# A two-block transformer forward on one core: scaling the pool weights and reordering the pool stage by hand, and two stacked norms from one power

## The chip, the cores and the metric

The kernel runs on one core of one Trainium2 chip. The metric is the device time of one execution in microseconds (us), the median over the runs shown. TensorE (PE) multiplies; VectorE (DVE), ScalarE (ACT) and GpSimd (POOL) work on tiles of 128 partitions; loads and stores are issued on the queue of SyncE (SP), a few on GpSimd's. The engines run at the same time and wait for each other by semaphores; each works through its own instructions in a fixed order, so an instruction that waits holds what stands behind it on the same engine.

## What is computed

256 tokens of 1024 numbers pass through two blocks. The first has a pooling layer and an attention layer, each followed by a gated feed-forward, and ends in an RMS norm. The second begins with a norm of its own, so two norms meet there.

```python
def rmsnorm(x, g):
    xf = x.astype(jnp.float32)
    y = xf * lax.rsqrt(jnp.mean(xf * xf, axis=-1, keepdims=True) + EPS)
    return (y * g.astype(jnp.float32)).astype(x.dtype)

def pool_mixer(h, w, scale):
    ...
    for g, win in enumerate(POOL_WINDOWS):          # (2, 4, 8, 16)
        ...
        outs.append(window_sum / cnt[None, :, None] - hf[:, :, sl])
    d = jnp.stack(outs, axis=2).astype(h.dtype)
    y = jnp.einsum('btgc,gce->btge', d, w).reshape(B, T, D)
    return y * scale

def first_block(x, norm_mixer, norm_ffn, pool_w, pool_scale, kv_norm, w_kv, w_q, w_o, rel_bias,
                w_gate_up, w_down, final_norm):
    ...
    for layer in range(DEPTH):                      # 2
        if layer < N_A_LAYERS:                      # 1
            x = x + pool_mixer(rmsnorm(x, norm_mixer[layer]), pool_w[layer], pool_scale[layer])
        else:
            ...
            x = x + o @ w_o[j]                      # attention
        x = x + swiglu(rmsnorm(x, norm_ffn[layer]), w_gate_up[layer], w_down[layer])
    return rmsnorm(x, final_norm)

def hybrid_layer(x, c, ...):                        # the second block
    ...
    h = rms_norm(x, norm1_g) * (1 + sc1) + sh1
    z = h @ w_in
    ...
```

The rest of the second block (sparse attention, a recurrent branch, a mixture of experts with 64 experts, a last norm) is not touched.

## The kernel before, in words

Tokens lie in two halves `t` of 128 partitions, `x_sb[:, t, :]`, and each half in two column halves `h` of 512. Large products are made in three parts: a weight is split into a high part `wH` (ScalarE copy, line 190 or 201) and a low part `wL` (a subtraction, line 191 on DVE, or line 202 on the engine that is handed in), the operand likewise (`hH`, `hL`), and `mm3` multiplies high by high, high by low, low by high (lines 206 to 208). Weights come into a ring of 1 MB buffers, `raw`, and a buffer can be loaded again once both parts of both column halves are split off.

The **pool stage** (lines 561 to 624) is the first stage. It loads `x`, the pooling matrix `am`, `vec` (gains and other columns), the pool weights `pw`, `k_base` (the identity for transposes), the first gate and up weights (`ffn0.load(0)`) and the scale row `psrow`, copied to all partitions, in this order on SP's queue. Then: the norm of each half (squares on ScalarE, two small DVE steps, a power to -0.5 on GpSimd that gives `rstd`, a scaling on DVE that gives `xn`); the pooling matmuls `pd`; their copies `dT` by ScalarE; the pool matmuls into `acc` (`pool_mm`); the update of `x_sb` (`pool_add`: multiply by `psrow`, add); the feed-forward's norm; transposes of `xn`; and the gain and split into `hH` (ScalarE) and `hL` (DVE) in `gain_split`. Here the order of ScalarE and DVE is as written (`manual_schedule`); that of TensorE, GpSimd and the queues is a planner's, which goes by its own estimates of time. `ffn0.prep(u, rest)` makes the high parts of unit `u` of the feed-forward (gate and up) and puts the low parts off into the list `rest`: entries 0 and 1 are unit 0, entries 2 and 3 unit 1. Before the change entries 0 and 1 run on DVE, 2 and 3 on GpSimd. `next(ada)` twice brings two of the matmuls of the second block's modulation between the transposes of the two halves.

The **feed-forward** (`Ffn.run`) goes through 22 units of 128 hidden columns: gate, up, the activation, and one unit later the product with `w_down` into four accumulators. Gate and up weights are loaded for two units at a time. `to_next` ends a stage: it adds the accumulators to `x_sb` (`upd`), takes the norm of each half, runs `mid` and transposes and spreads each half.

At the end of the **second feed-forward** (lines 739 to 804) both norms are made (`norm2`): sums of squares of `x`, the product `y` with the row `fr`, sums of squares of `y`, then two powers one after the other. Behind it stand the last modulation matmuls, `gains`, and a round trip of `gcol` and `bcol` through DRAM on GpSimd's queue (lines 801 to 804). GpSimd's next work there is loads and memsets for the second block, among them `ikz` (line 837), which the `pix` matmuls of line 899 need. `omu` (line 825) is a small DVE step on `vec` that the planner is free to place.

## Time and profile before

| | us |
|---|---|
| median of 3 runs | 1396.15 (1391.35 to 1396.72) |
| the profiled execution | 1396.91 |
| its span in the trace | 1394.8 |
| PE busy | 1338.2 (96%) |
| DVE busy | 743.8 (53%) |
| ACT busy | 548.3 (39%) |
| POOL busy | 118.8 (9%) |

An engine's busy time is a sum over the whole span, and PE matmuls overlap, so a PE at 96% is not a PE at its peak. A stage is read from the timeline of each engine over that stage: each row is a start, a duration, the instruction with what it writes and reads, and in brackets how long the engine was idle before it and what released it. The chain that ended last is the profile's own way back from the last instruction through what each step waited for.

### The profile page before, as it was taken

How to read it: one execution, taken by the hardware profiler on the slowest of the kernel's cores; microseconds unless marked ns; L12 is line 12 of the kernel's file. 1: busy time of each engine (PE TensorE's matmuls, PEld its weight loads, DVE VectorE, ACT ScalarE, POOL GpSimd, SP SyncE). 2: the span in 40 equal slices, each digit the busy share in tenths (PEclk: the TensorE clock that was granted, in tenths of full speed). 3: DMA queues.
4: the chain of work that ended last, by engine and by line, in shares of the span. 5: the costliest groups of instructions: out<-in, count | busy, mean ns of one | idle time of the engine just before them, and what ended most of it. 6: DMA issues, size and time to landing. Idle time of an engine off the chain costs nothing.

```text
span 1394.8 us, 22867 instructions
## 1 busy us (share of the span) xinstructions
PE 1338.2 (96%) x9151; PEld 1003.3 (72%) x9151; DVE 743.8 (53%) x1420; ACT 548.3 (39%) x1087; POOL 118.8 (9%) x158
## 2 busy tenths in 40 slices
PE   5999999999999998899999998899999999999996
PEld 4899997998799997789989888644545445445443
DVE  4656657565765555468777676533333343343333
ACT  4444445655544445365664543211221222222212
POOL 3010001000100002203342100300000000000000
PEclk9999999999999999899999998999999999999998
DMA  7887766652866646944411159499999999999993
GB/s 253 294 247 250 250 225 213 210 192 92 290 234 225 212 157 207 182 131 147 154 62 63 63 219 361 134 335 380 405 408 409 408 409 409 408 409 409 368 403 138
DMA packets 157312, 361.38 MB, mean 259 GB/s; under 512 B 9865, under 2 KB 92101, under 8 KB 153874
## 3 DMA queue, kind: packets, MB, share of 16 engines
q1 hardware_dynamic: 154674, 353.36, 70.0%
q0 software_dynamic: 2528, 6.51, 1.8%
q8 instruction: 75, 1.23, 0.4%
q14 instruction: 35, 0.29, 0.1%
HBM read 357.46 MB, written 2.37 MB: 258 GB/s over the span
## 4 chain that ended last, share of the span: by engine, by line
PE 79%; DMA 7%; issue 5%; DVE 5%; ACT 2%; POOL 1%; SPq 0%; POOLq 0%; ACTq 0%; DVEq 0%
PE pgu L1557 15%; PE pdn L1581 7%; PE pgu L206 5%; PE pgu L207 5%; PE pgu L208 5%; PE pxg L1524 4%; PE pz L206 4%; PE acc L1597 4%; PE pz L207 4%; PE pz L208 4%; PE acc L208 3%; PE acc L206 3%; PE acc L207 3%; DMA ew<-in_exp_up 3%; DMA raw<-in_w_gate_up 2%
## 5 line engine op out<-in xcount | busy, mean ns | idle before, releaser
L191 DVE TENSOR_TENSOR wL<-raw,wH 128x1024 fp32r<-128x1024 f32 (+1 forms) x229 | 270.7, 1186 | 200.2 <-ACT wH L190 199.4
L190 ACT ACTIVATE wH<-raw 128x1024 fp32r<-128x1024 f32 (+1 forms) x231 | 235.7, 1026 | 254.2 <-PE pgu L207 106.7
L207 PE MATMUL pgu<-hL,wH 128*128 128x256 f32 x704 | 198.1, 281 | 1.3 <-DVE hL L267 1.3
L206 PE MATMUL pgu<-hH,wH 128*128 128x256 f32 x704 | 198.0, 282 | 0.0
L208 PE MATMUL pgu<-hH,wL 128*128 128x256 f32 x704 | 198.0, 281 | 0.0
L207 PEld LDWEIGHTS pgu<-hL,wH 128*128 128x128 f32 x704 | 133.0, 189 | 3.5 <-DVE hL L267 1.7
L206 PEld LDWEIGHTS pgu<-hH,wH 128*128 128x128 f32 x704 | 132.7, 189 | 2.9 <-issue 0.6
L208 PEld LDWEIGHTS pgu<-hH,wL 128*128 128x128 f32 x704 | 133.0, 189 | 0.0
L206 PE MATMUL pz<-hH,wH 128*128 128x256 f32 x400 | 119.5, 299 | 3.3 <-ACT hH L190 2.6
L1557 PE MATMUL pgu<-ew,xx 128*64 128x512 f32 x512 | 117.8, 596 | 1.6 <-DMA ew<-in_exp_up 1.5
L1557 PE MATMUL pgu<-ew,xg 128*64 128x512 f32 x512 | 117.0, 596 | 0.4 <-DMA ew<-in_exp_up 0.4
L1581 PE MATMUL pdn<-ew,aT 128*64 128x512 f32 (+1 forms) x528 | 115.6, 580 | 0.0
L207 PE MATMUL pz<-hL,wH 128*128 128x256 f32 x400 | 114.3, 286 | 1.2 <-DVE hL L191 1.2
L208 PE MATMUL pz<-hH,wL 128*128 128x256 f32 x400 | 113.4, 284 | 0.0
L1581 PEld LDWEIGHTS pdn<-ew,aT 128*64 128x64 f32 x528 | 37.8, 137 | 72.1 <-issue 71.1
L1557 PEld LDWEIGHTS pgu<-ew,xx 128*64 128x64 f32 x512 | 36.2, 137 | 69.4 <-issue 66.1
L1557 PEld LDWEIGHTS pgu<-ew,xg 128*64 128x64 f32 x512 | 35.6, 137 | 67.4 <-issue 66.2
L1584 ACT ACTIVATE yH<-pdn 128x512 fp32r<-128x512 f32 (+1 forms) x66 | 38.5, 584 | 112.6 <-DVE pdn L1583 112.6
L206 PEld LDWEIGHTS pz<-hH,wH 128*128 128x128 f32 x400 | 76.6, 192 | 7.5 <-ACT hH L190 2.9
L207 PEld LDWEIGHTS pz<-hL,wH 128*128 128x128 f32 x400 | 76.7, 192 | 2.6 <-DVE hL L191 1.4
L208 PEld LDWEIGHTS pz<-hH,wL 128*128 128x128 f32 x400 | 76.6, 191 | 0.4 <-issue 0.3
L236 POOL TENSOR_TENSOR rstd<-ssv,mhalf 128x1 f32<-128x1 f32 x16 | 9.8, 614 | 768.0 <-DVE ssv L234 767.9
(408 smaller groups left out, 2528.1 us busy)
## 6 DMA issues: line engine op xcount, KB each, us to landing
ew<-in_exp_gate SPq DMA_DIRECT2D x128, 512.0 KB, 12.7
ew<-in_exp_up SPq DMA_DIRECT2D x128, 512.0 KB, 12.8
ew<-in_exp_down SPq DMA_DIRECT2D x64, 1024.0 KB, 12.1
raw<-in_w_gate_up SPq DMA_DIRECT2D x44, 1024.0 KB, 5.5
raw<-in_ada_w SPq DMA_DIRECT2D x24, 1024.0 KB, 5.0
raw<-in_w_in SPq DMA_DIRECT2D x23, 1024.0 KB, 5.3
raw<-in_w_down SPq DMA_DIRECT2D x22, 1024.0 KB, 5.3
raw<-in_w_kv SPq DMA_DIRECT2D x8, 1024.0 KB, 5.5
```

Source lines behind the costliest of these rows:

```text
L190: S.activation(dstH, src, AF.Copy)
L191: second.tensor_tensor(dstL, src, dstH.bitcast(F32), op=OP.subtract)
L206: PE.matmul(out_, lH, rH, start=first, stop=False)
L207: PE.matmul(out_, lH, rL, start=False, stop=False)
L208: PE.matmul(out_, lL, rH, start=False, stop=last)
L236: G.tensor_tensor(r, v, mhalf[:, 0:1], op=OP.pow)
L1524: PE.matmul(p[:, kk * w:kk * w + w], x[:, t, (kb + kk) * 128:(kb + kk) * 128 + 128], r, start=t == 0 and i == 0, stop=t == 1 and i == 1, s ...
L1557: PE.matmul(self.pg[64 * e:64 * e + 64, :].rearrange("p (i c) -> p i c", i=2), self.xg[:, k, 64 * e:64 * e + 64], self.W[e][k // 4][:, :, ...
L1581: PE.matmul(p[64 * e:64 * e + 64], self.aT[:, j, 64 * e:64 * e + 64], self.D[e][:, j, c:c + w], start=j == 0, stop=j == 1, skip_group_chec ...
L1584: S.activation(yH[:, sl], p, AF.Copy)
L1597: PE.matmul(self.ac[t][h][:, sl], l, self.y[h][i][:, sl], start=False, stop=i == 1 and self.last, skip_group_check=True)
```

## The change

Pool stage. The load of `psrow` moves from behind the gate/up loads to right behind `pw`. `pw` is multiplied by `psrow` in place, in two DVE instructions behind the second `xn`, so the accumulators hold the scaled result and the update of `x_sb` is one addition. ScalarE takes the squares of each half column by column behind its addition. The order is written out: both additions of half 0, the high parts of unit 0, its norm, then half 1's additions around the scaling of half 0, one low part, half 1's norm, both transposes; the high parts of unit 1 and the other three low parts follow behind these, all on DVE. `omu` is held behind the last low step of the last `gain_split`.

Second block. The update and the squares of `x` and `y` go by column halves as the accumulators come. Both norms come from one power over two columns: with v the mean square of `x` plus EPS, the second argument is the mean square of `y` over v, plus EPS.

```diff
-                    V.scalar_tensor_tensor(L[:, k, ts_], p[:, c], g(k), H[:, k, ts_].bitcast(F32), op0=OP.mult, op1=OP.subtract)
+                    last["gainL"] = V.scalar_tensor_tensor(L[:, k, ts_], p[:, c], g(k), H[:, k, ts_].bitcast(F32), op0=OP.mult, op1=OP.subtract).ins
...
         pw = wload(A["pool_w"].rearrange("o g (k p) e -> p (o g k) e", p=128), 8, 256)
+        psrow = wk.tile([128, D], F32, name="psrow")
+        DMA.dma_start(psrow, bcast(A["pool_scale"], D))
         K = consts(cp, "base")
         ident = K("ident")
         ffn0.load(0)
-        psrow = wk.tile([128, D], F32, name="psrow")
-        DMA.dma_start(psrow, bcast(A["pool_scale"], D))
...
+        pw = pw.rearrange("p (g k) e -> p g k e", k=2)
+        for k in range(2):
+            V.tensor_tensor(pw[:, :, k, :], pw[:, :, k, :], psrow.rearrange("p (g e) -> p g e", g=4), op=OP.mult)
...
-        def pool_add(t, h):
-            sl = x_sb[:, t, h * 512:(h + 1) * 512]
-            tmp = wk.tile([128, 512], F32, name="ptmp", bufs=2)
-            V.tensor_tensor(tmp, accs[t][h], psrow[:, h * 512:(h + 1) * 512], op=OP.mult)
-            V.tensor_tensor(sl, tmp, sl, op=OP.add)
-        rest = []
...
-        for t in range(2):
-            ffn0.prep(t, rest)
-            for h in range(2):
-                pool_add(t, h)
-                if t and not h:
-                    V.tensor_scalar(xn[:, 0, :], x_sb[:, 0, :], r0, None, op0=OP.mult)
-            sums = sumsq(x_sb[:, t, :], xn[:, t, :], "f0")
-            if t:
-                rest[1](V)
-                normed_t(1, xn, sums)
-                for f in rest[2:]:
-                    f(G)
-            else:
-                rest[0](V)
-                r0 = rsq(sums, "n")
-        for t in range(2):
-            if t:
-                with tc.issue_after(last["first"]):
-                    next(ada)
-                    next(ada)
-            transposed(xn, t, gain_split([(hH, hL, lambda k: vcol("nf0", k))], t))
+        rest, sums = [], [sm.tile([128, 2], F32, name="ss") for _ in range(2)]
+
+        def pool_add(t, h):
+            sl = slice(h * 512, (h + 1) * 512)
+            V.tensor_tensor(x_sb[:, t, sl], accs[t][h], x_sb[:, t, sl], op=OP.add)
+            S.activation(xn[:, t, sl], x_sb[:, t, sl], AF.Square, accum_out=sums[t][:, h:h + 1])
+
+        def scaled(t, r):
+            V.tensor_scalar(xn[:, t, :], x_sb[:, t, :], r, None, op0=OP.mult)
+        pool_add(0, 0)
+        pool_add(0, 1)
+        ffn0.prep(0, rest)
+        r0 = rsq(sums[0], "n")
+        pool_add(1, 0)
+        scaled(0, r0)
+        pool_add(1, 1)
+        rest[0](V)
+        r1 = rsq(sums[1], "n")
+        scaled(1, r1)
+        transposed(xn, 0, gain_split([(hH, hL, lambda k: vcol("nf0", k))], 0))
+        with tc.issue_after(last["first"]):
+            next(ada)
+            next(ada)
+        transposed(xn, 1, gain_split([(hH, hL, lambda k: vcol("nf0", k))], 1))
+        ffn0.prep(1, rest)
+        for f in rest[1:]:
+            f(V)
...
+        def upd2(t, h):
+
+            if not h:
+                ys.append(wk.tile([128, D], F32, name="y", bufs=2))
+                sums2.append([sm.tile([128, 2], F32, name="ss") for _ in range(2)])
+            sl = slice(h * 512, (h + 1) * 512)
+            add_acc(accs, t, h)
+            V.tensor_tensor(ys[t][:, sl], x_sb[:, t, sl], fr[:, sl], op=OP.mult)
+            for ss, src in zip(sums2[t], (x_sb[:, t, sl], ys[t][:, sl])):
+                S.activation(xn[:, t, sl], src, AF.Square, accum_out=ss[:, h:h + 1])
+
         def norm2(t):
 
-            y = wk.tile([128, D], F32, name="y", bufs=2)
-            s1 = sumsq(x_sb[:, t, :], xn[:, t, :], "fin")
-            V.tensor_tensor(y, x_sb[:, t, :], fr, op=OP.mult)
-            s2 = sumsq(y, xn[:, t, :], "w")
-            r1 = rsq(s1, "fin")
-            rr = sm.tile([128, 1], F32, name="rr")
-            V.tensor_tensor(rr, r1, r1, op=OP.mult)
-            V.tensor_scalar(s2, s2, rr, None, op0=OP.mult)
-            r2 = rsq(s2, "w")
-            V.tensor_scalar(xn[:, t, :], y, r1, r2, op0=OP.mult, op1=OP.mult)
-            S.activation(x_sb[:, t, :], y, AF.Copy, scale=r1)
+            y, vs = ys[t], wk.tile([128, 3], F32, name="vs2", bufs=2)
+            for i, ss in enumerate(sums2[t]):
+                V.tensor_scalar(vs[:, i:i + 1], ss[:, 0:1], ss[:, 1:2], 1.0 / D, op0=OP.add, op1=OP.mult)
+                if i:
+                    V.tensor_scalar(vs[:, 1:2], vs[:, 1:2], vs[:, 2:3], EPS, op0=OP.mult, op1=OP.add)
+                else:
+                    V.tensor_scalar(vs[:, 0:1], vs[:, 0:1], EPS, None, op0=OP.add)
+                    V.reciprocal(vs[:, 2:3], vs[:, 0:1])
+            rr = wk.tile([128, 2], F32, name="rr2", bufs=2)
+            G.tensor_tensor(rr, vs[:, 0:2], mhalf[:, 0:2], op=OP.pow)
+            V.tensor_scalar(xn[:, t, :], y, rr[:, 0:1], rr[:, 1:2], op0=OP.mult, op1=OP.mult)
+            S.activation(x_sb[:, t, :], y, AF.Copy, scale=rr[:, 0:1])
...
-            V.tensor_scalar(omu, vcol("mu"), -1.0, 1.0, op0=OP.mult, op1=OP.add)
+            with tc.issue_after(last["gainL"]):
+                V.tensor_scalar(omu, vcol("mu"), -1.0, 1.0, op0=OP.mult, op1=OP.add)
```

## Rows read from the trace of the kernel before

**Rows 1.** The page, part 4: the chain that ended last, shares by engine.

```profile
PE 79%; DMA 7%; issue 5%; DVE 5%; ACT 2%; POOL 1%; SPq 0%; POOLq 0%; ACTq 0%; DVEq 0%
```

**Rows 2.** Timeline of PE, 0 to 75 us: start, duration, instruction [idle before <-releaser].

```profile
14.44 0.66 PE L592 MATMUL acc<-raw,dT 128*128 128x256 f32 x2
...
18.93 4.05 PE L592 MATMUL acc<-raw,dT 128*128 128x256 f32 x18
29.79 1.94 PE L249 MATMUL pt<-k_base,xn 128*128 128x128 f32 x8 [6.81 <-DVE xn L609]
31.66 3.58 PE L513 MATMUL pada<-raw,silc 128*32 128x512 f32 x16
...
37.65 0.39 PE L207 MATMUL pgu<-hL,wH 128*128 128x256 f32 x1 [0.65 <-DVE hL L267]
...
52.56 0.28 PE L206 MATMUL pgu<-hH,wH 128*128 128x256 f32 x1
```

**Rows 3.** Waits of PE, 36 to 540 us: total, times, longest.

```profile
PE pt L249 <- DVE xn L241: 1.6, 2, 1.1
```

**Rows 4.** Timeline of DVE, 0 to 75 us.

```profile
7.98 0.17 DVE L825 TENSOR_SCALAR omu<-vec 128x14 f32<-128x14 f32 x1 [1.87 <-DMA vec<-in_vecs]
...
9.81 0.75 DVE L241 TENSOR_SCALAR xn<-x_sb,rstd 128x1024 f32<-128x1024 f32 x1 [0.67 <-POOL rstd L236]
18.92 0.69 DVE L598 TENSOR_TENSOR ptmp<-acc,psrow 128x512 f32<-128x512 f32 x1 [8.36 <-DMA psrow<-in_pool_scale]
19.64 0.69 DVE L599 TENSOR_TENSOR x_sb<-ptmp,x_sb 128x512 f32<-128x512 f32 x1
20.43 0.69 DVE L598 TENSOR_TENSOR ptmp<-acc,psrow 128x512 f32<-128x512 f32 x1
...
23.93 2.86 DVE L599 TENSOR_TENSOR x_sb<-ptmp,x_sb 128x512 f32<-128x512 f32 x1
...
32.97 2.30 DVE L241 TENSOR_SCALAR xn<-x_sb,rstd 128x1024 f32<-128x1024 f32 x1 [0.66 <-POOL rstd L236]
35.19 4.22 DVE L267 SCALAR_TENSOR_TENSOR hL<-pt,vec,hH 128x128 fp32r<-128x128 f32 x16
```

**Rows 5.** Timeline of POOL, 0 to 75 us.

```profile
6.19 0.56 POOL L236 TENSOR_TENSOR rstd<-ssv,mhalf 128x1 f32<-128x1 f32 x1 [2.67 <-DVE ssv L234]
...
23.89 5.09 POOL L202 TENSOR_TENSOR wL<-raw,wH 128x1024 fp32r<-128x1024 f32 x2
...
32.88 1.84 POOL L695 MEMSET qz<- 128x1024 f32 x2
```

**Rows 6.** The chain that ended last, 530 to 620 us: start, duration, what.

```profile
552.04 16.41 DMA gain_scr<-bcol
...
569.33 11.62 DMA gain_scr<-gcol
...
586.58 1.22 PE pix L899 x2
```

**Rows 7.** Waits of PE, 540 to 1395 us.

```profile
PE pix L899 <- ACT ikz L852: 4.1, 1, 4.1
```

**Rows 8.** The load of `pw`: SP's timeline, the issues (to landing), the stretch 10 to 12.

```profile
2.62 0.63 SPq L186 DMA_DIRECT2D raw<-in_pool_w  x1
...
raw<-in_pool_w SPq DMA_DIRECT2D x1, 1024.0 KB, 8.3
...
10.00:12.00 2.00, 1.51 (x7) 1.33 (x6) 0.56 (x1) 0.47 (x1) 0.00 (x0) 1.00 1.08 357
```

**Rows 9.** The page, part 5: low and high parts, busy us and mean ns.

```profile
L191 DVE TENSOR_TENSOR wL<-raw,wH 128x1024 fp32r<-128x1024 f32 (+1 forms) x229 | 270.7, 1186 | 200.2 <-ACT wH L190 199.4
L190 ACT ACTIVATE wH<-raw 128x1024 fp32r<-128x1024 f32 (+1 forms) x231 | 235.7, 1026 | 254.2 <-PE pgu L207 106.7
```

**Rows 10.** Windows: length, busy of PE, PEld, DVE, ACT, POOL, then PEclk, DMA, GB/s.

```profile
29.00:35.00 6.00, 5.21 (x24) 2.16 (x24) 5.27 (x7) 2.78 (x10) 2.33 (x3) 0.50 0.12 18
```

**Rows 11.** The page, part 6: gate/up loads, KB each, us to landing.

```profile
raw<-in_w_gate_up SPq DMA_DIRECT2D x44, 1024.0 KB, 5.5
```

More of the change, by code (lines that the diff above doesn't have):

```diff
@@ L592, in pool_mm @@
                     PE.matmul(accs[t][h][:, (g % 2) * 256:(g % 2) * 256 + 256], dT[:, 2 * g + kk, t * 128:(t + 1) * 128],
-                              pw[:, 2 * g + kk, :], start=kk == 0, stop=kk == 1)
-        def pool_add(t, h):
-            sl = x_sb[:, t, h * 512:(h + 1) * 512]
-            tmp = wk.tile([128, 512], F32, name="ptmp", bufs=2)
-            V.tensor_tensor(tmp, accs[t][h], psrow[:, h * 512:(h + 1) * 512], op=OP.mult)
-            V.tensor_tensor(sl, tmp, sl, op=OP.add)
-        rest = []
+                              pw[:, g, kk, :], start=kk == 0, stop=kk == 1)
         for t in range(2):
@@ L760, in build @@
         xn = xnorm(es)
-        def norm2(t):
-            y = wk.tile([128, D], F32, name="y", bufs=2)
-            s1 = sumsq(x_sb[:, t, :], xn[:, t, :], "fin")
-            V.tensor_tensor(y, x_sb[:, t, :], fr, op=OP.mult)
-            s2 = sumsq(y, xn[:, t, :], "w")
-            r1 = rsq(s1, "fin")
-            rr = sm.tile([128, 1], F32, name="rr")
-            V.tensor_tensor(rr, r1, r1, op=OP.mult)
-            V.tensor_scalar(s2, s2, rr, None, op0=OP.mult)
-            r2 = rsq(s2, "w")
-            V.tensor_scalar(xn[:, t, :], y, r1, r2, op0=OP.mult, op1=OP.mult)
-            S.activation(x_sb[:, t, :], y, AF.Copy, scale=r1)
+        ys, sums2 = [], []
+        def upd2(t, h):
[7 more added lines that the diff above has]
+                S.activation(xn[:, t, sl], src, AF.Square, accum_out=ss[:, h:h + 1])
+        def norm2(t):
+            y, vs = ys[t], wk.tile([128, 3], F32, name="vs2", bufs=2)
[10 more added lines that the diff above has]
+            S.activation(x_sb[:, t, :], y, AF.Copy, scale=rr[:, 0:1])
         def spread2(t):
@@ L793, in mid @@
             pa2.close()
-        to_next(tail, lambda t, h: add_acc(accs, t, h), norm2, spread2, ada, mid=mid)
+        to_next(tail, upd2, norm2, spread2, ada, mid=mid)
     for _ in ada:
```

## The prediction, made before the result was known

> **What bounds the kernel now.** I read the chain that ended last first: TensorE holds 79% of it, DVE 5%, DMA 7% [rows 1]. So an edit to DVE or GpSimd work pays only where TensorE waits for it, and the next view is TensorE's own waits. Up to 36 us TensorE has two holes [rows 2]: nothing before the first `xn` (8.8 us), and 6.81 us idle behind the last pool matmul until the normalised tile `xn` of line 609 comes. The first feed-forward matmul that runs without a break is the one at 37.65. From there to 540 us its listed waits are all short, 1.6 us at the most [rows 3]. Hence the time of that matmul sets the rest of the first block: what the pool stage gives up there arrives later one for one, since the loads behind it start when earlier buffers come free and move along.
>
> In the second hole DVE is the long engine. It waits 8.36 us for `psrow`, starts at 18.92 and then has no gap until 32 [rows 4]. Steps there are far longer than their own kind: the add at 23.93 takes 2.86 us where the one at 19.64 takes 0.69, the scaling at 32.97 takes 2.30 where the one at 9.81 takes 0.75. GpSimd runs at exactly these times: two low parts for 5.09 us, then two memsets of `qz` for 1.84 us [rows 5]. A DVE step that meets a long GpSimd step ends about when that ends.
>
> The second place of the change is the end of the second feed-forward, 542 to 587 us. There the chain does not run over TensorE: it goes from GpSimd's last `rstd` into the write of `bcol`, its landing 16.41 us later, the write of `gcol`, 11.62 us, and on to the clearing of `ikz` and the `pix` matmul at 586.58 [rows 6]. TensorE had reached `pix` 4.1 us before [rows 7].
>
> **Front of the pool stage.** `omu` waits 1.87 us for `vec` and holds the first `xn` until 8.07 [rows 4]; its `rstd` is done at 6.19 + 0.56 = 6.75 [rows 5]. With `omu` behind a much later instruction, `xn` runs from 6.85, the second norm follows at the same distances, and the second `xn` ends near 9.35 instead of 10.56: 1.2 us. The `pd` matmuls are released by `xn` in both halves, so they follow.
>
> **The new wait.** The matmuls now need `pw` scaled by `psrow`. The `psrow` load moves ahead of `k_base` and the two gate/up loads on SP's queue. `pw` is issued at 2.62 and lands 8.3 us later, 10.9; if loads land in the order of their issue, 512 KB more at the 357 GB/s of that stretch is 1.5 us, so `psrow` lands near 12.4 [rows 8], where DVE now has it at 18.9 [rows 4]. Everything it is moved past comes 1.5 us later: `k_base` (first used by the transposes after 24) and the two gate/up loads, whose first use on ScalarE is after 22 us in either order. Two multiplies of 128x1024 with both inputs in SBUF stand nearest to DVE's low parts of that size, 1.19 us each at the mean [rows 9]: `pw` is ready at 14.8, the first pool matmul runs at 14.95 where it ran at 14.44. Behind the first multiply, on DVE, nothing is queued but the stage's own adds. TensorE's order is the planner's and I can't see it. If it stays as it is (pool matmuls between the `pd` ones), the whole pool sequence comes 0.5 us later, and the last wait of the front turns from `dT` to `pw`; if all `pd` go first, they fill the wait.
>
> **From the sums to the first matmul, order as now.** The second sum of the first half is ready at 20.43 + 0.5 = 20.9. One add of 0.69 takes the place of multiply and add (4 x 0.69 saved). Then: add to 21.65; ScalarE's squares to 22.4; two small DVE steps 22.85; `rstd` 23.45; add 23.6; scaling; add 25.05; low part 26.2; the small steps 26.6; `rstd` 27.2. ScalarE meanwhile has squares, two high parts (1.03 each [rows 9]) and squares, done 25.9, ahead of its use. The second scaling is 0.75 alone, 2.30 under the memsets. The memsets stood right behind the last `rstd` [rows 5] and nothing in the diff moves them, so I take 2.30: 29.55. Then eight low steps of the first half, 4.22 / 16 = 0.264 each [rows 4], 31.65, and the first of the second half: TensorE runs without break from about 32.0. Saved: 37.65 - 32.0 = 5.65 us. Other work there is hidden: the first transposes at 24.5, the ada matmuls behind the first gain (26.3; 3.58 us at worst, to 29.9 [rows 2]), the second transposes then wait for `xn` all the same. The granted clock behind the hole of 6.81 us was 0.50, the level of 1.2 GHz [rows 10]; with holes of 1 us it should stay at the high one, which only widens that cover.
>
> The Trainium skill, "SBUF — State Buffer", section "SBUF: two separate sides", gives a rule for the long steps: the DVE/GpSimd port pair is an exclusive lock, held for the whole instruction by whichever starts first, and a memset counts as a GpSimd operation. That speaks against part of this change, since the low parts leave GpSimd but the memsets stay. The rows agree (2.30 and 0.75). By the rule the sum is the 5.65 above; without it 1.55 more.
>
> **The moved low parts.** Of the four, three now stand on DVE behind the second half's low steps, ending near 35.0, 36.2, 37.4. TensorE reaches the up half of unit 0 at 32.0 + 2.9 and unit 1 at 37.8, so they are just in time: 0 to 0.3 us. But the gate/up buffers are free only then, and the next gate/up loads can leave only at 36.3 and 37.5, 4.3 and 5.5 us into the feed-forward. One takes 5.5 us to land at the median [rows 11], so they land some 10 and 11 to 12 us into it; unit 2 begins 14.9 us in (52.56 - 37.65 [rows 2]). Splitting takes 1.03 on ScalarE and 1.19 on DVE [rows 9]; 1 to 3 us are left, so nothing is lost. If that cover is gone, TensorE waits for what is missing at unit 2.
>
> **Both norms from one power.** Per half the change drops one `rstd`, `rr` and the scaled sum, and adds a reciprocal (one more of DVE's small steps, ahead of the last square) and separate halves of `y`. After the last square only two small steps, one power and the scaling are left; the second `xn` comes some 2 us earlier. TensorE starts the `pz` matmuls perhaps 1.5 to 2 us earlier, and then waits that much longer at `pix`. What counts is when GpSimd issues the `bcol` write: 34.5 us of fixed DMA and queue follow it. It left at 552.04, right behind a power [rows 6]. Bounds: the copy slips in front of the last power, 550.3 (gain 1.7); the order stays, 551.95 (0.1); the copy falls behind the scaling on DVE, 553.2 (loss 1.2). I take 0.9, from the first two.
>
> **Sum.** The profiled execution took 1396.91 us (span 1394.8), 0.76 above the median 1396.15. 1396.91 - 5.65 - 0.9 = 1390.4; against the median that is 1389.6, which I forecast. With the bounds of the `bcol` write, and 1 us either way for the hops between engines that the walk rounds, this case spans 1387.8 to 1392.7.
>
> **Rivals.**
> All `pd` before the pool matmuls: the sum of the first half is complete at 14.95 + 2 x 8 x 0.22 = 18.45 (18 took 4.05 [rows 2]), not 20.9, and 2.45 us more are saved: 1387.2. For it: `pw` is late, so a list in order of readiness would fill with `pd`. Against: a planner that takes loads for shorter than they are sees no gap.
> The memsets fall elsewhere: 1.55 us more, 1388.1 alone, 1385.6 with the one before. This is what would hold if the lock rule did not meet them. Against: GpSimd is in order and had them right behind the last `rstd`.
> The change is swallowed at the edges: the stall at `pix` takes its part, the planner puts later work (sums of the ada rows on DVE) ahead of the low parts, and half the gain goes: 1392 to 1396.
> The other side: `psrow` lands late. It is read as 128 copies of one row, and if it again needs 18.9, `pw` is ready at 21.3, the pool matmuls (32 x 0.22 = 7) end at 28.3 with TensorE idle for 5 us before, partly at the low clock (up to 7 more). Every step above moves by 6.4 to 10, and the first matmul comes at 38.5 to 42: 1396 to 1400. It decides from a landing of about 18, where the 5.65 us are gone; for it speaks only that late landing now, against it that two 1 MB loads stood before it there.
>
> **How the numbers follow.** About 0.5% (7 us) is what a measurement of this kernel can tell from no change: faster means under 1389.2. Forecast 0.42: 0.18 under that line, 0.24 over it. All `pd` first 0.22 and memsets elsewhere 0.10, both faster. Swallowed 0.15, same. Late `psrow` 0.08: 0.05 same, 0.03 slower by over 0.5%, where the loads of unit 2 are missed besides. What I don't see of the planner's order 0.03, slower. Faster 0.50, same 0.44, slower 0.06. The range reaches from the first two rivals together with the larger `bcol` gain, 1385.6 - 0.8 and a little below, 1384, to the start of the last one, 1396.
>
> **What would show it.** `psrow` landing between 11.5 and 14 and `pw` scaled by 15; no DVE step over 1.3 us before 26 and one of 2.3 at the memsets; no TensorE hole over 2 us after 15; a first unbroken feed-forward matmul at 29.5 to 32.5 us; no wait at unit 2; the `bcol` write 0.1 to 1.7 us earlier against the end of the second feed-forward, and still a wait at `pix`, as long or longer than 4.1 us. The forecast is wrong if the shift at 37.65 isn't found again at the expert stage, or if loads of the feed-forward hold TensorE.

## The result, and the profile of the changed kernel

The changed kernel takes 1379.36 us (median; 1372.24 to 1381.69) where the kernel before, run on the same chip, takes 1396.09: a ratio of 0.9879 [0.9836, 0.9922]. The forecast was 1389.6, with a range from 1384 to 1396. The direction was right and the gain, 16.7 us, is more than twice the forecast's 6.5. Its profiled execution took 1380.44 us, with a span of 1378.7, 16.1 below that of before.

The pool stage first. The timeline of PE in the changed kernel answers to [rows 2]: start, duration, instruction, [idle before <-releaser].

```profile
7.71 1.30 PE L584 MATMUL pd<-k_amat,xn 128*128 128x144 f32 x4 [7.71 <-DVE xn L241]
...
13.43 0.70 PE L596 MATMUL acc<-raw,dT 128*128 128x256 f32 x2 [0.86 <-DVE raw L590]
...
18.19 4.05 PE L596 MATMUL acc<-raw,dT 128*128 128x256 f32 x18
24.85 1.67 PE L249 MATMUL pt<-k_base,xn 128*128 128x128 f32 x8 [2.61 <-DVE xn L610]
26.45 2.94 PE L513 MATMUL pada<-raw,silc 128*32 128x512 f32 x16
29.32 1.10 PE L249 MATMUL pt<-k_base,xn 128*128 128x128 f32 x8
...
31.60 0.39 PE L207 MATMUL pgu<-hL,wH 128*128 128x256 f32 x1 [0.77 <-DVE hL L267]
```

The hole of 6.81 us behind the last pool matmul is down to 2.61, and the first unbroken feed-forward matmul starts at 31.60 where it started at 37.65: 6.05 us, of the 16.1. The forecast had 32.0 and 5.65. The same stretch on DVE, answering to [rows 4], and the memsets on POOL, answering to [rows 5]:

```profile
8.60 0.75 DVE L241 TENSOR_SCALAR xn<-x_sb,rstd 128x1024 f32<-128x1024 f32 x1 [0.67 <-POOL rstd L236]
12.14 2.36 DVE L590 TENSOR_TENSOR raw<-raw,psrow 128x1024 f32<-128x1024 f32 x2 [2.80 <-DMA psrow<-in_pool_scale]
...
19.69 0.69 DVE L606 TENSOR_TENSOR x_sb<-acc,x_sb 128x512 f32<-128x512 f32 x1 [2.83 <-PE acc L596]
...
22.29 2.30 DVE L610 TENSOR_SCALAR xn<-x_sb,rstd 128x1024 f32<-128x1024 f32 x1
...
27.29 0.75 DVE L610 TENSOR_SCALAR xn<-x_sb,rstd 128x1024 f32<-128x1024 f32 x1 [0.67 <-POOL rstd L236]
27.96 2.15 DVE L267 SCALAR_TENSOR_TENSOR hL<-pt,vec,hH 128x128 fp32r<-128x128 f32 x8
31.20 2.16 DVE L267 SCALAR_TENSOR_TENSOR hL<-pt,vec,hH 128x128 fp32r<-128x128 f32 x8 [1.08 <-ACT hH L263]
33.27 3.49 DVE L202 TENSOR_TENSOR wL<-raw,wH 128x1024 fp32r<-128x1024 f32 x3
```

```profile
22.20 1.84 POOL L699 MEMSET qz<- 128x1024 f32 x2
```

`psrow` is there at 12.14, and the two multiplies end at 14.50. The one long DVE step, 2.30 us, again stands beside the memsets, but it is the scaling of the first half, not of the second.

The other ten microseconds lie behind 31.60. The waits of TensorE from 36 to 540 us (total, times, longest) are as short as in [rows 3]:

```profile
PE pt L249 <- DVE xn L241: 1.5, 2, 1.1
PE acc L208 <- DVE aL L191: 1.4, 2, 0.8
```

So no wait went away there, and yet the two feed-forwards got shorter, from the first unbroken matmul to the last of the gate and up halves: 179.88 to 176.70 us and 179.84 to 176.98, 6.0 us together. The activation of ScalarE (line 415) marks each unit of the feed-forward. Its timeline in the kernel before, two rows seven units apart:

```profile
136.63 0.36 ACT L415 ACTIVATE silu<-pgu 128x256 f32<-128x256 f32 x1
...
196.07 0.36 ACT L415 ACTIVATE silu<-pgu 128x256 f32<-128x256 f32 x1
```

and in the changed kernel, also seven units apart:

```profile
128.54 0.36 ACT L415 ACTIVATE silu<-pgu 128x256 f32<-128x256 f32 x1
...
187.14 0.37 ACT L415 ACTIVATE silu<-pgu 128x256 f32<-128x256 f32 x1
```

Seven units took 59.44 us and take 58.60: 8.491 and 8.371 us a unit, 0.12 less, over 44 units 5.3 us. The work is the same. From start to start, two neighbouring matmuls into `pgu` stood 118.6 ns apart (118.7 from the seventh unit on) and stand 116.8 (means over the starts in the trace between 80 and 200 us). This start-to-start time is called the pitch from here on. It isn't the clock; the windows from 40 to 210 us (length, busy of PE, PEld, DVE, ACT, POOL, then granted clock, DMA share, GB/s), the kernel before and then the changed one:

```profile
40.00:210.00 170.00, 169.71 (x1209) 158.26 (x1208) 102.10 (x110) 74.72 (x100) 5.74 (x10) 1.00 0.76 251
```

```profile
40.00:210.00 170.00, 170.00 (x1223) 159.10 (x1222) 103.09 (x111) 78.04 (x103) 5.73 (x10) 1.00 0.74 249
```

The granted clock is 1.00, the level of 2.4 GHz, in both; the changed kernel gets 14 more matmuls into the same 170 us.

**The cause put forward.** The diff drops the tile `rr`, four buffers of 32 bytes a partition in the pool of small tiles. Everything allocated behind it moves down by 128 bytes: `raw`, `wH` (54080 to 53952) and `wL`, while the operands `hH` (212960) and `hL` (221152), which are allocated from the other end, stay. These addresses are those of the build; the traces hold none. The theory is that the place of the buffers sets the pitch of the matmuls. The rivals: the new pool stage or the new norms shorten the feed-forward in some other way, or it is a property of one execution.

The end of the second feed-forward, the chain that ended last, answering to [rows 6] (start, duration, what):

```profile
539.98 14.10 DMA gain_scr<-bcol
...
554.96 12.38 DMA gain_scr<-gcol
...
572.98 0.70 PE pix L918 x2
```

The last product of that feed-forward starts at 547.69 before and at 536.83 after. Counted from there the `bcol` write leaves at 3.15 us where it left at 4.35, and `pix` starts at 36.15 where it started at 38.89. Of these 2.7 us, 1.2 are the earlier write and the rest a faster round trip in this execution. With the 6.0 us of the feed-forwards that makes 8.7 of the ten; the other 1.3 us lie in no one place that is read here.

### The profile page after: what moved, and what is told of

Read it like the earlier page. It is cut to its first block, busy times and chain, and to the rows that moved or that the text cites. A ratio compares the mean times of both kernels' runs of the same rounds, so it can differ in the third digit from the quotient of the medians.

```text
span 1378.7 us, 22859 instructions
## 1 busy us (share of the span) xinstructions
PE 1330.8 (97%) x9151; PEld 996.2 (72%) x9151; DVE 741.4 (54%) x1420; ACT 548.4 (40%) x1087; POOL 112.9 (8%) x154
## 4 chain that ended last, share of the span: by engine, by line
PE 81%; DMA 7%; issue 5%; DVE 4%; ACT 2%; POOL 1%; SPq 0%; POOLq 0%; ACTq 0%; DVEq 0%
PE pgu L1576 15%; PE pdn L1600 7%; PE pgu L207 6%; PE pgu L206 6%; PE pgu L208 6%; PE pxg L1543 4%; PE pz L206 4%; PE acc L1616 4%; PE pz L207 4%; PE pz L208 4%; PE acc L208 3%; PE acc L206 3%; PE acc L207 3%; DMA ew<-in_exp_up 3%; DMA gain_scr<-bcol 1%
## 5 line engine op out<-in xcount | busy, mean ns | idle before, releaser
L1576 PE MATMUL pgu<-ew,xx 128*64 128x512 f32 x512 | 118.3, 596 | 1.5 <-DMA ew<-in_exp_up 1.5
L207 PE MATMUL pz<-hL,wH 128*128 128x256 f32 x400 | 113.7, 284 | 0.9 <-DVE hL L191 0.9
L1603 ACT ACTIVATE yH<-pdn 128x512 fp32r<-128x512 f32 (+1 forms) x66 | 38.5, 584 | 112.6 <-DVE pdn L1602 112.6
L208 PE MATMUL acc<-wH,aL 128*128 128x512 f32 x176 | 69.3, 395 | 1.4 <-DVE aL L191 1.4
```

Source lines behind the costliest of these rows:

```text
L207: PE.matmul(out_, lH, rL, start=False, stop=False)
L208: PE.matmul(out_, lL, rH, start=False, stop=last)
L1576: PE.matmul(self.pg[64 * e:64 * e + 64, :].rearrange("p (i c) -> p i c", i=2), self.xg[:, k, 64 * e:64 * e + 64], self.W[e][k // 4][:, :, ...
L1603: S.activation(yH[:, sl], p, AF.Copy)
```

## The experiments

**One part at a time.** Four kernels take the change apart. First the place alone (e1): the kernel before, with `rr` in another pool, so that the buffers stand where the changed kernel has them.

```diff
-            rr = sm.tile([128, 1], F32, name="rr")
+            rr = wk.tile([128, 1], F32, name="rr", bufs=2)
```

> The kernel before with one edit: the two small tiles rr of the stacked norms lie in the stage's own pool instead of the pool of small tiles, which is 128 bytes shorter for it, so all weight buffers behind it start 128 bytes lower, as in the changed kernel; no instruction is added, dropped or moved by it in the source. Theory of place: the unit of a feed-forward takes 8.37 us instead of 8.48 and the matmul pitch is 116.8 ns instead of 118.7, both feed-forwards together 4 to 6 us shorter, time 1388 to 1393. Theory of runs (the pitch is a matter of the execution, not of the program): pitch 118.7 or anything else, without relation to the edit, time 1391 to 1397. Theory of the planner (other orders bring the units closer): unit 8.48, time 1394 to 1398.

Measured: 1388.61 us (before 1395.26), ratio 0.9954 [0.9937, 0.9971]. Seven units take 58.60 us, as in the changed kernel:

```profile
136.08 0.37 ACT L415 ACTIVATE silu<-pgu 128x256 f32<-128x256 f32 x1
...
194.68 0.37 ACT L415 ACTIVATE silu<-pgu 128x256 f32<-128x256 f32 x1
```

No instruction is added or removed, and 6.6 us are gone. The two feed-forwards hold 4.3 of them in the trace (2.2 and 2.1); the rest lies in other stages, where one trace can't tell it from the spread of executions. The interval of the ratio reaches from 4.0 to 8.8 us, so that it could be no more than the 4.3.

Then the new pool stage (e2) with `omu` held back, with the old second block and the buffers in their old place:

```diff
+        psrow = wk.tile([128, D], F32, name="psrow")
+        DMA.dma_start(psrow, bcast(A["pool_scale"], D))
         K = consts(cp, "base")
...
+        for k in range(2):
+            V.tensor_tensor(pw[:, :, k, :], pw[:, :, k, :], psrow.rearrange("p (g e) -> p g e", g=4), op=OP.mult)
```

> The pool stage's part and the held back omu alone, the second block as before; the buffers lie where they lay. Expected of the stage: the first unbroken feed-forward matmul at 31.6 us instead of 37.65, 6.05 us. Theory of place: units at 8.48 us, time 1396 - 6 = 1390 (1388 to 1392). If the pool stage itself makes the units shorter (other order of loads or low parts): units at 8.37, 1386 to 1388.

Measured: 1388.03 us, 0.9952 [0.9934, 0.9969], pitch 118.7 ns: 7.2 us for the pool stage, with the old pitch and within the range of the theory of place. In its profiled execution the first unbroken feed-forward matmul starts only at 33.95, behind front matmuls that ran at half pace for longer (below).

The second block's norms alone (e3: the `upd2` and `norm2` of the change in the kernel before; `rr` goes with them, so the buffers move as well):

```diff
-            rr = sm.tile([128, 1], F32, name="rr")
-            V.tensor_tensor(rr, r1, r1, op=OP.mult)
...
+            G.tensor_tensor(rr, vs[:, 0:2], mhalf[:, 0:2], op=OP.pow)
```

> The second block's part alone: update and squares by halves, both norms from one power; rr is gone, so the buffers lie 128 bytes lower. Expected of the norms themselves: pix starts about 2.9 us earlier counted from the last accumulator matmul of the second feed-forward (35.9 us instead of 38.9 behind it), and 2.4 us more by the last pix. Theory of place: units at 8.37 as well, time 1396 - 5 - 5 = 1386 (1383 to 1390). Theory of runs or planner: units at 8.48, time 1390 to 1393.

Measured: 1385.86 us, 0.994 [0.9921, 0.9959], pitch 116.8 ns. That is 2.7 us under the place alone, but the two intervals overlap. In its trace `pix` starts 38.35 us behind the last product and not 35.9: the forecast of 2.9 us for the norms, taken from the first trace of the changed kernel, was not met.

The changed kernel with its buffers put back at 54080 (e4):

```diff
-        v = sm.tile([128, 1], F32, name="ssv")
+        v = sm.tile([128, 16], F32, name="ssv")[:, 0:1]
```

> The changed kernel with one edit: the small tiles ssv are 64 bytes long instead of 4, of which 4 are used, so that the weight buffers lie 128 bytes higher, where they lay before the change. Theory of place: units at 8.48 us, matmul pitch 118.7 ns, 4 to 6 us slower than the changed kernel: 1383 to 1387. Theory of runs: as the changed kernel within its spread, 1376 to 1382, whatever the pitch.

Measured: 1387.95 us, 0.9952 [0.9933, 0.9971]; a microsecond above its range; seven units take 59.44 us again:

```profile
128.52 0.36 ACT L415 ACTIVATE silu<-pgu 128x256 f32<-128x256 f32 x1
...
187.96 0.37 ACT L415 ACTIVATE silu<-pgu 128x256 f32<-128x256 f32 x1
```

The whole code change without the move is worth 7.3 us, close to the forecast's 6.5. And a second measurement of the changed kernel itself (e8):

> The changed kernel once more, beside its variants of this call. Its weight buffers begin at an address that leaves 192 bytes over a multiple of 512 (before the change 320 over). Theory of place: matmul pitch 116.8 ns in the feed-forwards as in its first trace, time 1376 to 1383. Theory of runs: another pitch.

Measured: 1380.68 us (before 1394.38), 0.9892 [0.986, 0.9924], seven units 58.60 us. So it is no property of one execution: the pitch goes with the place, and neither with the new pool stage nor with the new norms.

**Other places.** Three kernels move the weights of the changed kernel by the size of another small tile, and nothing else (e5 by 64 bytes up, e6 by 64 down, e7 by 192 down):

```diff
-    mx = sm.tile([128, 1], F32, name="cmx", bufs=1)
+    mx = sm.tile([128, 24], F32, name="cmx", bufs=1)[:, 0:1]
```

> The changed kernel with one small tile enlarged, so that the weight buffers lie 64 bytes higher (256 over a multiple of 512). If the pitch follows the start of the weights within 512 bytes step by step: between 116.8 and 118.7 ns, time 2 to 3 us above the changed kernel. If multiples of 128 or 256 are what counts: below 116.8, time below the changed kernel.

```diff
-            ws = sm.tile([128, 1], F32, name="ws")
+            ws = sm.tile([128, 1], F32, name="ws", bufs=2)
```

> The changed kernel with two buffers fewer for a small tile, so that the weight buffers lie 64 bytes lower (128 over a multiple of 512). If the pitch follows the distance step by step: some 115.8 ns, 2 to 3 us below the changed kernel. If multiples of 128 count: as much below as the variant 64 bytes higher. If only the two places seen so far differ by chance: 116.8 or 118.7.

```diff
-        n8 = sm.tile([128, 8], F32, name="n8")
+        n8 = sm.tile([128, 8], F32, name="n8", bufs=2)
...
-            wr = sm.tile([128, 1], F32, name="wr")
+            wr = sm.tile([128, 1], F32, name="wr", bufs=2)
```

> The changed kernel with fewer buffers for three small tiles, so that the weight buffers lie 192 bytes lower, at a multiple of 512. If being in line with 512 is best: pitch near 110 to 114 ns and 8 to 18 us below the changed kernel. If it is only the place against the operands hH and hL, which lie 480 over such a multiple in all kernels: no better than the variant 64 bytes lower.

Measured: 1383.84, 1388.85 and 1383.06 us (ratios 0.9915 [0.9886, 0.9945], 0.997 [0.9952, 0.9988], 0.9912 [0.9886, 0.9938]). The pitches are 118.25, 120.1 and 118.25 ns: two places 256 bytes apart have the same pitch, and a move of 64 bytes down is worse than the place of before. Seven units with the weights 64 bytes lower:

```profile
130.48 0.36 ACT L415 ACTIVATE silu<-pgu 128x256 f32<-128x256 f32 x1
...
190.16 0.36 ACT L415 ACTIVATE silu<-pgu 128x256 f32<-128x256 f32 x1
```

59.68 us. The ideas put forward for these runs fell: e5 alone would fit steps along the address, but e6 goes the other way; a multiple of 512 is not best; and e7 is better than e6. What the two equal places suggest is that it repeats every 256 bytes.

Two more places, 32 bytes up and 32 down, and one kernel that leaves the weights and moves the operands (e9, e11 and e10):

```diff
-    mx = sm.tile([128, 1], F32, name="cmx", bufs=1)
+    mx = sm.tile([128, 16], F32, name="cmx", bufs=1)[:, 0:1]
```

> The changed kernel with the weight buffers 32 bytes higher (wH at 53984 instead of 53952; the operands hH and hL stay at 212960 and 221152). Modulo 256 the places measured so far are 0, 64, 128 and 192, and the pitch of the feed-forward's matmuls there 118.25, 118.7, 120.1 and 116.8 ns; this one is 224, which is also that of hH. Theory A (the place of the weights modulo 256 alone sets the pitch, and it goes evenly between the measured places): between 116.8 and 118.25, near 117.5, and 1.5 to 2 us more than the changed kernel's 1380, about 1382. Theory B (what counts is that weights and operand differ in their place modulo 256, and equal places are best): below 116.8, and 1380 or less. Theory C (equal places are worst, since both reads fall on the same part of the memory): 120 or more, 1386 to 1389.

```diff
+    V.memset(open_pool(feed, "gap", side="right").tile([128, 16], F32, name="gap"), 0.0)
     fp = open_pool(feed, "feed", side="right")
```

> The changed kernel with its weights where they are (53952, 192 modulo 256) and the feed-forward's operands hH and hL moved 64 bytes lower (212896 and 221088, 160 modulo 256), by an unused tile of 64 bytes at the far end of the memory, which costs one short DVE memset at the start. Theory A (the weights' place alone): pitch 116.8 ns as in the changed kernel, 1380 +- 2 us. Theories B and C (the distance between weights and operand): the distance goes from 32 to -32 modulo 256, the pitch changes by 1 ns or more in either direction, and the time by 3 us or more.

```diff
-            ws = sm.tile([128, 1], F32, name="ws")
+            ws = sm.tile([128, 1], F32, name="ws", bufs=3)
```

> The changed kernel with the weight buffers 32 bytes lower (wH at 53920, 160 modulo 256; operands as they were). Theory A with even steps between the measured places: between 116.8 (192) and 120.1 (128), near 118.4 ns, about 1384 us. If only the class of 64 bytes counts (a place is good or bad by the 64-byte row in which a buffer starts), 160 falls with 128: 120.1 ns and 1387 to 1389 us. Theory B (distance to the operand, 64 here as it is 96 at 128 and 32 at 192): between the two as well, so this run tells the even steps from the classes, and e9 and e10 tell A from B.

Measured: 32 up 1389.54 us, 0.9968 [0.9953, 0.9982], 119.7 ns; operands moved 1386.37, 0.9947 [0.9928, 0.9967], 118.25 ns; 32 down 1382.1, 0.9918 [0.9897, 0.994], 117.8 ns. Even steps between places (theory A for the first) gave 117.5 and fell; theory B (equal places best) fell with them, and theory C (120 or more) came within 0.3 ns. 32 down lies nearer to the even steps (118.4) than to the 120.1 of the classes. The texts of e10 and e11 count the distance from the weights to the operand; here and in the table below it is the weights less the operand, the other sign. With the weights untouched, moving the operands (and what else is allocated from that end) cost 1.4 ns a matmul and some 6 us:

```profile
128.22 0.36 ACT L416 ACTIVATE silu<-pgu 128x256 f32<-128x256 f32 x1
...
187.57 0.37 ACT L416 ACTIVATE silu<-pgu 128x256 f32<-128x256 f32 x1
```

59.35 us, exactly that of the two kernels with pitch 118.25 above. All three have the weights 32 bytes above the operand, modulo 256. That suggested the distance.

**Distance or place.** The changed kernel with both moves that were bad alone, weights 64 bytes down and operands 64 bytes down (f2):

```diff
+    V.memset(open_pool(feed, "gap", side="right").tile([128, 16], F32, name="gap"), 0.0)
...
+            ws = sm.tile([128, 1], F32, name="ws", bufs=2)
```

> The changed kernel with the weight buffers 64 bytes lower (wH at 53888, as in e6_m64) and the operands 64 bytes lower as well (hH at 212896, as in e10_right64). Each of the two moves alone made the kernel slower: pitch 120.1 and 118.25 ns, 1388.9 and 1386.4 us. Distance theory (what counts is the place of weights less the place of operand, modulo 256): the distance is -32 again, as in the changed kernel, so the pitch returns to 116.8 ns, the down product's to 230.3 ns, and the time to 1380 +- 2 us. Theory of the weights' place alone: 120.1 ns and 1388 to 1390 us. If each move costs by itself: over 121 ns and 1393 us or more.

Measured: 1383.49 us (1378.31 to 1386.13; before 1395.79), 0.9907 [0.9878, 0.9937], pitch 116.8 ns, the down product's 230.2, as in the changed kernel:

```profile
130.83 0.37 ACT L416 ACTIVATE silu<-pgu 128x256 f32<-128x256 f32 x1
...
189.43 0.37 ACT L416 ACTIVATE silu<-pgu 128x256 f32<-128x256 f32 x1
```

58.60 us: the best pitch is back, to the hundredth. The median is 3 us above the changed kernel's and 1.5 above the range, but the intervals overlap, and its profiled execution is one of the two with the longest half-paced front (below). By the pitch the distance theory holds and that of the weights' place alone falls. On the kernel before, weights 128 down and operands 64 down (f1):

```diff
+    V.memset(open_pool(feed, "gap", side="right").tile([128, 16], F32, name="gap"), 0.0)
...
+            rr = wk.tile([128, 1], F32, name="rr", bufs=2)
```

> The kernel before with its weights 128 bytes lower, as in e1_shift, and the operands 64 bytes lower: nothing of the change's pool stage or norms. Distance theory: +32, as in e5_p64, e7_m192 and e10_right64, pitch 118.25 ns, so most of the 6.6 us of e1_shift go again: 1393 to 1395. Weights alone: 116.8 ns and 1388.6 as in e1_shift.

Measured: 1392.45 us, 0.9984 [0.9972, 0.9996], 118.25 ns. The pitch is as the distance says, and half of the 6.6 us of e1 is gone again, with 3.3 left; the time is half a microsecond below the range of 1393 to 1395. The two distances that were missing (f3 and f4):

```diff
-    mx = sm.tile([128, 1], F32, name="cmx", bufs=1)
+    mx = sm.tile([128, 32], F32, name="cmx", bufs=1)[:, 0:1]
```

> The changed kernel with the weight buffers 96 bytes higher (wH at 54048, operands as they were): the distance to the operand is +64 modulo 256, one of two not measured yet. No theory has a number for it; between those of +32 (118.25 ns) and +96 (118.7 ns) if the map is smooth there, about 1384 to 1388 us. It would be worth keeping if it falls below 116.8.

```diff
+            ws = sm.tile([128, 1], F32, name="ws", bufs=2)
...
+            wr = sm.tile([128, 1], F32, name="wr", bufs=3)
```

> The changed kernel with the weight buffers 96 bytes lower (wH at 53856): distance 128 modulo 256, the last of the eight steps of 32 bytes. Its neighbours -96 (160) and +96 have 120.1 and 118.7 ns; if the map is smooth there, 119 to 120 ns and 1386 to 1390 us.

Measured: 1378.96 us, 0.9887 [0.9859, 0.9915], and 1388.87, 0.9949 [0.9929, 0.9969]. The first was forecast at 1384 to 1388 and can't be told from the changed kernel, so no version beats it; the second is in its range, with 118.6 ns instead of 119 to 120. All of them together, with the place of `wH` less that of `hH` modulo 256, the pitch in either feed-forward, and seven units of the first (of the kernels with the old pool stage, before has +96, e1 and e3 have -32, and f1 has +32):

| distance | pitch, first ns | pitch, second ns | seven units us | kernels: median us |
|---|---|---|---|---|
| -96 | 120.1 | 120.1 | 59.68 | e6 1388.9 |
| -64 | 117.8 | 117.8 | 59.11 | e11 1382.1 |
| -32 | 116.8 | 116.6 to 116.7 | 58.60 | changed 1379.4, 1380.7; e12 1380.7; f2 1383.5 |
| 0 | 119.7 | 119.8 | 59.77 | e9 1389.5 |
| +32 | 118.25 | 118.3 | 59.35 | e5 1383.8; e7 1383.1; e10 1386.4 |
| +64 | 117.8 | 115.7 | 59.11 | f3 1379.0 |
| +96 | 118.7 | 118.5 to 118.6 | 59.44 | e2 1388.0; e4 1388.0 |
| 128 | 118.6 | 119.9 | 59.40 | f4 1388.9 |

From the seventh unit of the first feed-forward on the pitch goes with the distance, with no plain shape; the time follows the mean of the two feed-forwards. But the distance doesn't fix the pitch. At +64 and 128 the second feed-forward differs from the first, though its operands lie in the same buffers. At +64 it even changes from unit to unit, 113.7 ns in one and 117.8 in the next, as the activations of f3 show:

```profile
416.45 0.36 ACT L415 ACTIVATE silu<-pgu 128x256 f32<-128x256 f32 x1
...
424.88 0.37 ACT L415 ACTIVATE silu<-pgu 128x256 f32<-128x256 f32 x1
...
433.16 0.36 ACT L415 ACTIVATE silu<-pgu 128x256 f32<-128x256 f32 x1
```

One unit takes 8.43 us, the next 8.28. So one and the same place can have two paces, and the place decides which ones occur. That the place of the buffers sets the time is shown; what happens inside the memory, and what chooses between two paces, is left open.

**The sum.** Last the new pool stage and the place together, without the new norms (e12), that is e2 with

```diff
-            rr = sm.tile([128, 1], F32, name="rr")
+            rr = wk.tile([128, 1], F32, name="rr", bufs=2)
```

> The kernel before with the new pool stage and omu held back, its old second block, and the tile rr taken out of the pool of small tiles (it stands in the pool wk), so that the weight buffers stand 128 bytes lower, as in the changed kernel. It differs from the changed kernel only in the second block. If the three parts simply add, this is 1395 less 7.2 (the pool stage alone) less 6.6 (the place alone), 1381, pitch 116.8 ns, and the new norms are worth 0 to 1 us. If the norms carry the 2.7 us by which the second block alone went below the place alone, it is 1383. By the forecast's term of 0.9 us for the norms it is between, 1381 to 1382.

Measured: 1380.71 us (before 1394.47), 0.9903 [0.9878, 0.9928]. The two parts add up: 7.2 + 6.6 is 13.8, measured 13.8. The changed kernel, which has the norms besides, was 1379.36 and 1380.68. So the times can't tell what the norms are worth: 0.1 us between e2 and e4, 0 to 1.4 here, 2.7 between e1 and e3, all within the intervals, with the forecast's 0.9 among them. The traces say a little more: the `bcol` write leaves 3.1 to 3.3 us behind the last product in all thirteen with the new norms and 4.3 to 4.4 in all five with the old, and `pix` starts 37.6 us behind it at the mean (36.1 to 38.6) instead of 38.5 (37.6 to 39.2).

## Why the prediction was wrong, point by point

**The step that failed** is the costing of "drops one `rstd`, `rr` and the scaled sum" in the part on both norms. `rr` was counted as an instruction and not as a tile. The sum has no term for where the buffers go, and it took for granted that behind 37.65 us everything only moves along. That term measured 6.6 us alone (e1) and 6.5 beside the new pool stage (the gain of e12, 13.8, less that of e2, 7.2). Forecast 1389.6 less 6.6 is 1383.0, and the intervals of both measurements of the changed kernel (1373.2 to 1385.2 and 1374.9 to 1383.8) contain that. No row of before gave a price for the place; but that the move exists could be read from the diff and the tiles' sizes, and the range should then have had a term of unknown size on the 2112 gate and up matmuls of the two feed-forwards. None of the rivals had TensorE itself running faster, so none could catch it.

**The pool stage came out right in size, in part by luck.** 5.65 us were forecast and 6.05 found in the trace. Over the fourteen traces with the new stage the first unbroken matmul lies between 30.08 and 33.95 us, against 37.65 to 38.15 in the four with the old one, so one trace alone would bear 3.7 to 8. `psrow` was forecast to land at 12.4 and was there at 12.14; the scaled `pw` at 14.8 was there at 14.50. The first pool matmul came a microsecond earlier than before and not 0.5 later (13.43): the first two need only the first of the two multiplies. TensorE's order around the pool matmuls stayed, so the rival with all `pd` first fell, and so did the one in which `psrow` lands at 18.9. The luck is in the path: the addition that completes the first half ended at 20.38 and not 21.65, the second `xn` at 28.04 and not 29.55, and TensorE gave most of this back, as follows.

**The memsets** were forecast on the second scaling and hit the first. GpSimd has nothing to do between the two `rstd`, and the planner put them there: a DVE step of 2.30 us stands before 26, where the prediction's signs allowed none over 1.3. The rule of exclusive access cited in the prediction (the Trainium skill, "SBUF — State Buffer", section "SBUF: two separate sides") agrees with both rows: 2.30 us beside the memsets, 0.75 without. The second `xn` was done at 28.04 and not at 29.55, yet the transposes start at 29.32: the wait did not go, its owner changed. The modulation matmuls (`pada`), forecast as hidden, stand before them until 29.39. Here the hole mattered as well. It was 2.61 us, not the 1 forecast, over the 2 that the prediction's signs allowed, and the granted clock fell behind it; the windows of the changed kernel, columns as above:

```profile
24.80:26.40 1.60, 1.55 (x8) 1.30 (x8) 1.60 (x3) 1.12 (x4) 0.00 (x0) 0.61 1.00 412
26.40:29.40 3.00, 3.00 (x18) 0.68 (x18) 2.30 (x9) 1.66 (x7) 0.55 (x1) 0.64 0.10 38
29.30:31.00 1.70, 1.51 (x13) 1.05 (x9) 0.81 (x4) 0.98 (x4) 0.00 (x0) 1.00 0.88 212
```

A granted clock of 0.61 and 0.64 is a mixture of the levels of 1.2 and 2.4 GHz, [rows 10] had 0.50. The sixteen `pada` matmuls take 2.94 us here; elsewhere on PE's timeline of the same trace, where the granted clock is 1.00, sixteen take 1.92:

```profile
538.74 1.92 PE L513 MATMUL pada<-raw,silc 128*32 128x512 f32 x16
```

The trace of e5 tells what that costs. On DVE it has the same times (`xn` at 22.29 and 27.29 us) and before the transposes the same hole of 2.61, but the granted clock stays at 1.00 behind it:

```profile
25.84 1.92 PE L513 MATMUL pada<-raw,silc 128*32 128x512 f32 x16
28.19 1.06 PE L249 MATMUL pt<-k_base,xn 128*128 128x128 f32 x8 [0.43 <-ACT hH L263]
...
30.43 0.39 PE L207 MATMUL pgu<-hL,wH 128*128 128x256 f32 x1 [0.78 <-DVE hL L267]
```

```profile
26.40:29.40 3.00, 2.55 (x25) 1.14 (x17) 2.30 (x9) 2.20 (x10) 0.55 (x1) 1.00 0.47 126
```

The first unbroken matmul is at 30.43 there and at 31.60 in the changed kernel, so the fall of the clock costs 1.2 us. It stays up in four of the fourteen traces (e4, e5, e9 and e10, first unbroken matmul at 30.08 to 30.43) and falls in the other ten (31.60 to 33.95), behind a hole of 2.61 to 2.64 us in all of them; what decides between the two is not shown.

**The low parts** went as forecast: three on DVE to 36.76 us, no wait at unit 2, none above 1.1 us until 540.

**The norms.** The `bcol` write left 1.2 us earlier, inside the bounds of 0.1 to 1.7 (0.9 was taken), since only one power stands in front of the copy now, where three did, and the last one behind it. But `pz` did not start earlier: 11.64 us behind the last product where it was 11.50. The waits of TensorE there before:

```profile
PE pz L206 <- ACT hH L190: 2.6, 1, 2.6
PE pt L249 <- DVE xn L773: 1.7, 1, 1.7
```

and in the changed kernel, answering to [rows 7]:

```profile
PE pz L206 <- ACT hH L190: 4.3, 1, 4.3
PE pix L918 <- ACT ikz L871: 0.8, 1, 0.8
```

The second `xn` comes 1.5 us earlier (4.91 us behind the last product instead of 6.41), and TensorE then waits that much longer for `hH`: 4.3 us in one place instead of 1.7 and 2.6 in two. ScalarE is what is late next: it starts the last scaling of `x_sb` 4.91 us behind the last product (4.80 before), then makes two high parts of weights, 1.99 us, and only then the first `hfull`, in both kernels. The wait at `pix` was forecast at 4.1 or longer and was 0.8, but in the second trace of the changed kernel it is:

```profile
PE pix L918 <- ACT ikz L871: 3.0, 1, 3.0
```

That trace has `pix` 38.16 us behind the last product, 0.7 less than before, where the first one had 36.15: the two round trips through DRAM vary by 2 us between executions of one kernel. The prediction called the way from the `bcol` write to `pix` fixed, at 34.5 us; over the eighteen traces it takes 33.0 to 35.4, more than the gain that was to pass through it. Another such stretch, from the last `pT` to the first `pxg`, took 133.3 us in one trace of the changed kernel and 128.9 in the other (133.4 before). So the gap of two single spans isn't to be divided up to the last microsecond; the medians of kernels with one part each bear more.

## What to carry to other kernels

A tile taken away or resized is also a change of every address behind it. Where TensorE runs without waits, compare the pitch of equal matmuls in both traces before any of the gain is put down to the code; a kernel with a padding tile of the same size tells the two apart. A gain on one engine ends where another becomes the late one: name the engine that is late next, here ScalarE with two weight copies in front of the spreading.

## What the hardware showed that was not expected

- The start-to-start time of back-to-back 128x128 by 128x256 matmuls, at a granted clock of 1.00, went from 116.8 to 120.1 ns with the distance modulo 256 between the stationary and the moving operand's addresses, and was the same to 0.1 ns in every trace of a distance (first feed-forward, from the seventh unit on). Two operands with equal places modulo 256 are among the slowest (119.7). At a distance of +64 every other unit of the second feed-forward ran at 113.7. The Trainium skill ("TensorE: Matmul & The Clock Gate", section "Back-to-back issue gap") has the spacing of such a stream set by weight load and matmul together, and names no address there. The table of that section of the Trainium skill, for an isolated matmul, has 262 cycles for 256 columns, an estimate of 109 ns at 2.4 GHz; every pitch measured here lies above that.
- At the start the matmuls run at half pace for a time that differs between executions. In the trace of e2, two `pd` matmuls at 15 us and two at 18:

```profile
15.16 0.68 PE L584 MATMUL pd<-k_amat,xn 128*128 128x144 f32 x2
...
18.28 0.41 PE L584 MATMUL pd<-k_amat,xn 128*128 128x144 f32 x2
```

In the changed kernel the fast pace is there by 11.93 us (0.41 for two), in the kernel before by 14.94. The record of the granted clock in each trace begins, with 1.00, where the pace doubles: at 17.92 us in e2, 11.49 in the changed kernel, 14.57 before. For the time ahead of that it holds nothing, and the 1.00 that a window shows there (as that of [rows 8], from 10 to 12 us) is not a reading. Half the pace is what the level of 1.2 GHz would give, but no record names the level. The two traces in which it lasts longest (e2 and f2, where the record begins at 17.50) reach the first unbroken feed-forward matmul 2.3 us after the changed kernel's first trace.
- By the chain that ended last, a write of `bcol` and one of `gcol` to DRAM (4 KB each) took 14.10 and 12.38 us to land in the changed kernel's first trace, 15.52 and 12.98 in its second, and 16.41 and 11.62 before [rows 6], from the same queue.
